# Expert w_down loads in 8 KB runs with every-second-column transposes, 4 KB of DMA scratch, and a fifth ring3 block

## The chip, the cores and the metric

The kernel runs on one core of a Trainium2 chip. The metric is the device time of one execution in microseconds (us), as the median of several runs; the profile is of one such execution. The core's engines are named as in the profile: PE (matmuls) with its weight loads PEld, DVE, ACT, POOL and SP. SP does no arithmetic here: its queue issues most of the DMAs, strictly one after the other. A "q" behind an engine's name (SPq, POOLq) marks what its sequencer issues or waits for.

## What is computed

One layer of a hybrid decoder for 512 prompt tokens and 32 sample tokens: RMSNorm, one input projection, dilated attention, a convolution module, attention into 256 memory tokens, a gated merge with output projection, and then a mixture of 32 experts with top-1 group and top-2 experts in it. Everything up to the experts is the same before and after, so only the last part of the reference is given:

```python
D_MODEL, N_EXPERTS, EXPERT_FF = 1024, 32, 512

def hier_moe(h, lw):
    lg = h @ lw['w_router_group'] + lw['b_router_group']
    pg = softmax(lg); pg_top, g_idx = top_k(pg, 1)
    le = einsum('nd,gde->nge', h, lw['w_router_expert']) + lw['b_router_expert']
    pe = softmax(le of the chosen group); pe_top, e_idx = top_k(pe, 2)
    w = pg_top * pe_top / sum(pe_top)
    gates = one_hot(g_idx * 8 + e_idx) weighted by w          # (544 tokens, 32 experts)
    y = zeros_like(h)
    for e in range(N_EXPERTS):
        hid = silu(h @ lw['w_expert_gate'][e]) * (h @ lw['w_expert_up'][e])
        y = y + gates[:, e:e + 1] * (hid @ lw['w_expert_down'][e])
    return y
```

All data are 32-bit floats. The weights of one expert are 1024x512 (gate), 1024x512 (up) and 512x1024 (down), 2 MB each.

## The kernel before

The kernel runs the whole layer up to the output projection first (the mixer), then the routing, then the 32 experts. Each expert takes up to 64 tokens; tokens beyond that would go to a loop at the end (`For_i` over `n_ovf`), which in the profiled execution makes no pass.

**Weights.** `expert_w(e, alloc)` takes six blocks of [128, 2048] floats (1 MB each) and loads into them, in this order, two halves of gate, two of up and two of down (g0, g1, u0, u1, d0, d1). Loads are numbered through here: load 6e is g0 of expert e, load 6e + 5 its d1, and 191 is the last. A gate or up block gives each partition four rows of 512 floats that lie together in memory, one run of 8 KB. A down block gives partition p the rows p and p + 128 of its half of w_down: two runs of 4 KB.

**Blocks.** `mraw()` hands out blocks in a fixed round: 4 of `ring2`, 2 of `ring2b`, 1 of `ring2c`, 6 of `ring`, 4 of `ring3` (in the order `ORD3`), 2 of `ring4`, 2 of `ring5`, 21 in all. So load j can be issued only when load j - 21 has been read for the last time by PE. The pools of `ring3`, `h2`, `ring4` and `ring5` lie one on top of the other on the left side of SBUF, over space that the mixer has left.

**Queue of loads.** `wload` (through `chained`, L573) issues all loads on the SP queue in their order, and its manual dependency (`DEPTH = 4`) makes each load wait until the load four places before it has landed. So at most four loads are in flight.

**One expert** (`expert_mm`): 32 matmuls with the gate blocks into `pg` and 32 with the up blocks into `pu` (L1477); the gather of the next expert's tokens (`chosen`, `gather`: L1296, two sets of PE work, L1301); silu and product into `hs` (L1485, L1486); two PE transposes of `hs` into `ph` (L1489); a copy to `hT` (L1491); 16 matmuls with the down blocks into `pd` (L1495); scaling by the gates into `o` (L1498); and a scatter with addition of 128 half rows into the output, issued by POOL (L1499).

**Overflow tables.** Before expert 14, `overflow_tables()` takes one more block, `scr`, from `ring` alone, so it gets the next block of those six in turn. About 35 DVE instructions (from L1522) work in it and write `novf` (L1530). `nc.values_load(novf...)` then loads that number into a register of every engine, SP included; in the trace SP's part of it shows as L1576.

**Order.** The order of the instructions within each queue is fixed when the kernel is built, by a planner that follows the program with a simulated clock (`TCKW = dict(schedule_with_timeline_sim=True)`); loads stay in their order, but what stands between two of them on SP is the planner's choice. `YENG` puts two of the output stores on SP as well (L1206).

Of the kernel before, what the change touches and what calls it, by code (L numbers as in the profile page):

```python
# [21 lines left out]
P = 128  # L22
# [28 lines left out]
RING2 = 4  # L51
RING2B = 2
RING2C = 1
RING3 = 4
RING4 = 2
RING5 = 2
SPOS = 2
# [7 lines left out]
DEPTH = 4  # L65
NBUSY = (50, 4)
GORD = (4, 0, 1, 2, 3)
ORD3 = (0, 3, 1, 2)
AHJ = 1
NGH = 3  # L70
MVT = {0: "hi"}
# [82 lines left out]
def build(tc, I, O, cols):  # L154
    nc = tc.nc
    stack = ExitStack()

    def pool(name, bufs=1, space=None, side="left"):
        kw = dict(name=name, bufs=bufs, reuse_waits="tile")
        if space is not None:  # L160
            kw["space"] = space
        else:
            kw["side"] = side
        return tc.tile_pool(**kw)
# [16 lines left out]
    ident = cp.tile([P, P], F32, name="ident")  # L181
# [7 lines left out]
    def cfs(k):  # L189
        a, n = cf_cols[k]  # L190
        return cf[:, a - CF0:a - CF0 + n]
# [7 lines left out]
    def nm(s):  # L199
        cnt[0] += 1  # L200
        return f"{s}_{cnt[0]}"
# [369 lines left out]
    def chained(dst, src):  # L571
        with tc.issue_after(last_load[0].ins):
            last_load[0] = nc.sync.dma_start(dst, src)  # L573
# [221 lines left out]
    for b in range(DB):  # L795
# [14 lines left out]
        for h in range(4):  # L810
            r = slice(32 * h, 32 * h + 32)
            q = [qm[:, 4 * g + h, :] for g in range(3)]
            nc.tensor.matmul(psA[r], q[1], KT[h], start=False, stop=last, skip_group_check=True)
        for h in range(4):
            r = slice(32 * h, 32 * h + 32)
            q = [qm[:, 4 * g + h, :] for g in range(3)]
            nc.tensor.matmul(psB[r, 0:P], q[0], KT[h][:, 384:], start=False, stop=False, skip_group_check=True)
        for h in range(4):
            r = slice(32 * h, 32 * h + 32)
            q = [qm[:, 4 * g + h, :] for g in range(3)]  # L820
# [351 lines left out]
    for q in range(4):  # L1172
        wh, wl = split(ounits[q])
        for ip in range(2):
# [5 lines left out]
            for g in ([slice(0, 2)] if not SPL[q][ip] else [slice(0, 1), slice(1, 2)]):  # L1180
# [9 lines left out]
                for c in range(2):  # L1190
                    k = 2 * q + c
# [17 lines left out]
    ring3 = moe.enter_context(pool("ring3", 1))  # L1209
    first = {"w%d" % q: ring3.tile([P, 2048], F32, name=nm("w"), tag="w%d" % q) for q in range(RING3)}  # L1210
    h2pool = moe.enter_context(pool("h2", 1))
# [71 lines left out]
    def pick(dst, col):  # L1283
        return V.tensor_tensor(dst, col.to_broadcast([P, 5, CAP]), cfs("iota64").unsqueeze(1).to_broadcast([P, 5, CAP]),
                               op=ALU.is_equal)
# [51 lines left out]
    for v in range(2):  # L1337
        px = mm.tile([P, 2, P], F32, name=nm("mm"), tag="mm")
        for i in GORD:
            for f in range(2):  # L1340
                k = 4 * v + 2 * f
# [68 lines left out]
    wg, wu, wd = I["w_expert_gate"][0], I["w_expert_up"][0], I["w_expert_down"][0]  # L1410
# [3 lines left out]
    def mraw():  # L1414
        q = seq[0] % (RING + RING2 + RING2B + RING2C + RING3 + RING4 + RING5)
        seq[0] += 1
        pl = ring
        for cand, n in ((ring2, RING2), (ring2b, RING2B), (ring2c, RING2C), (ring, RING), (ring3, RING3), (ring4, RING4), (ring5, RING5)):
            if q < n:
                pl = cand  # L1420
                break
            q -= n
        tag = "w%d" % ORD3[q] if pl is ring3 else "w"
        if tag in first:
            return first.pop(tag)
        return pl.tile([P, 2048], F32, name=nm("w"), tag=tag)
# [3 lines left out]
    def wload(dst, src):  # L1430
        chained(dst, src)
        loads.append(last_load[0].ins)
        if len(loads) > DEPTH:
            tc.add_manual_dep(loads[-1], loads[-1 - DEPTH].name,
                              mybir.DependencyInfo(mybir.DependencyClass.Sync, mybir.DependencyReason.DATA),
                              reason="bounded queue")

    def expert_w(e, alloc):
        out = []
        for src in (wg, wu):  # L1440
            for f in range(2):
                t = alloc().rearrange("p (k c) -> p k c", k=4)
                wload(t, src[e].rearrange("(p k) c -> p k c", k=8)[:, 4 * f:4 * f + 4, :])
                out.append(t)
        for f in range(2):
            t = alloc().rearrange("p (k c) -> p k c", k=2)
            wload(t, wd[e].rearrange("(k p) c -> p k c", p=P)[:, 2 * f:2 * f + 2, :])
            out.append(t)
        return out

    def gathered(oh):
        gather(oh, lambda: pm.tile([P, 512], F32, name=nm("px"), tag="px", bufs=1), xg, xT1)
        return xT1
# [6 lines left out]
    def expert(xT, w, gc, idc2, after=None, mid=None, early=None):  # L1460
        with tc.issue_after(after.ins) if after is not None else nullcontext():
            return expert_mm(xT, w, gc, idc2, mid, early)
# [8 lines left out]
    def expert_mm(xT, w, gc, idc2, mid, early):  # L1471
        pgt = pm.tile([P, 256], F32, name=nm("pg"), tag="pg")
        pup = pm.tile([P, 256], F32, name=nm("pu"), tag="pu")
        for ps, ws in ((pgt, w[0:2]), (pup, w[2:4])):
            for k in range(8):
                for f in range(2):
                    last = nc.tensor.matmul(ps[CAP * f:CAP * f + CAP], xT[:, k, :], ws[k // 4][:, k % 4, 256 * f:256 * f + 256],  # L1477
                                     start=(k == 0), stop=(k == 7))
            if early is not None and ps is pgt:
                early(last)  # L1480
        if mid is not None:
            with tc.issue_after(last.ins):
                mid()
        hs = work[:, 512:768]
        nc.scalar.activation(hs, pgt, AF.Silu)  # L1485
        nc.vector.tensor_tensor(hs, hs, pup, op=ALU.mult)  # L1486
        ph = pm.tile([P, 2, P], F32, name=nm("ph"), tag="ph", bufs=1)
        for f in range(2):
            nc.tensor.transpose(ph[:, f, :], hs[:, f * P:(f + 1) * P], ident)  # L1489
        hT = work[:, 768:1024].rearrange("p (f s) -> p f s", f=2)  # L1490
        nc.vector.tensor_copy(hT, ph)  # L1491
        pd = pm.tile([P, 512], F32, name=nm("pd"), tag="pd")
        for kk in range(4):
            for f in range(2):
                last = nc.tensor.matmul(pd[CAP * f:CAP * f + CAP], hT[:, kk % 2, CAP * (kk // 2):CAP * (kk // 2) + CAP],  # L1495
                                 w[4 + kk // 2][:, kk % 2, 512 * f:512 * f + 512], start=(kk == 0), stop=(kk == 3))
        o = work[:, :512]
        nc.vector.tensor_scalar(o, pd, gc, None, op0=ALU.mult)  # L1498
        nc.gpsimd.indirect_dma_start(out=y2, out_offset=bass.IndirectOffsetOnAxis(ap=idc2, axis=0), in_=o,  # L1499
                                     in_offset=None, compute_op=ALU.add)  # L1500
        return last
# [66 lines left out]
    for e in range(NE):  # L1568
        w = expert_w(e, mraw)
        if e == 14:  # L1570
            overflow_tables()
        done = expert(xTs[e], w, gates[:, e:e + 1], ids2[:, e:e + 1], done,
                      (lambda: xTs.append(chosen(e + 1))) if e + 1 < NE else None,
                      tables if e == 0 else None)

    n_ovf = nc.values_load(novf[0:1, 0:1], min_val=0, max_val=MAXOVF)  # L1576
    with tc.For_i(0, n_ovf, 1) as it:
        ev = nc.sync.value_load(ovfe[0:1, ds(it, 1)], min_val=0, max_val=NE - 1)
        idc2 = wk.tile([P, 1], I32, name="oidc2")
        gc = wk.tile([P, 1], F32, name="ogc")  # L1580
        nc.vector.tensor_copy(idc2, ids2[:, ds(it + NE, 1)])
        nc.vector.tensor_copy(gc, gates[:, ds(it + NE, 1)])

        def oraw():
            return ring.tile([P, 2048], F32, name=nm("w"), tag="w")

        out = []
        for src in (wg, wu):
            for f in range(2):
                t = oraw().rearrange("p (k c) -> p k c", k=4)  # L1590
                nc.sync.dma_start(t, src[ds(ev, 1)].rearrange("o (p k) c -> p (o k) c", k=8)[:, 4 * f:4 * f + 4, :])
                out.append(t)
        for f in range(2):
            t = oraw().rearrange("p (k c) -> p k c", k=2)
            nc.sync.dma_start(t, wd[ds(ev, 1)].rearrange("o (k p) c -> p (o k) c", p=P)[:, 2 * f:2 * f + 2, :])
            out.append(t)
        oe = wk.tile([P, 2], F32, name="oe")
        nc.vector.tensor_copy(oe[:, 0:1], ovff[:, ds(it, 1)])
        nc.vector.tensor_copy(oe[:, 1:2], ovfb[:, ds(it, 1)])
        oe1 = wk.tile([P, 32], F32, name="oe1")  # L1600
        pc5 = wk.tile([P, 5, 32], F32, name="pc5")
        pc = wk.tile([P, 5, 1], F32, name="pc")
        nc.vector.tensor_scalar(oe1, cfs("iotab")[:, :32], oe[:, 0:1], None, op0=ALU.is_equal)
        nc.vector.tensor_tensor(pc5, posE, oe1.unsqueeze(1).to_broadcast([P, 5, 32]), op=ALU.mult)
        nc.vector.tensor_reduce(pc[:, :, 0], pc5, AX.X, ALU.add)
        nc.vector.tensor_scalar(pc, pc, oe[:, 1:2], None, op0=ALU.subtract)
        oh = ohs[:, 0]
        pick(oh, pc)
        expert(gathered(oh), out, gc, idc2)
# [34 lines left out]
```

## Time and profile before

| | |
|---|---|
| median of 3 runs (lowest, highest) | 1234.89 us (1234.37, 1235.35) |
| span of the profiled execution, first to last instruction | 1233.3 us |
| mean granted TensorE clock | 0.990 of full speed |
| DMA traffic of the execution | 313.02 MB in 125575 packets |
| busy share of the span: PE, PEld, DVE, ACT, POOL | 94%, 69%, 39%, 25%, 24% |

The profile gives no separate device time for the profiled execution; the runs lie 1.1 to 2.1 us above its span. A busy share is a mean over the whole span, and stages differ: the first 640 us are the mixer, the experts' loads begin at 640.7 us and the first scatter of an expert is at 753.8 us. In the tables below "x" is a count; in a row of waits stand the time in all, the number of waits and the longest.

### The profile page before, as it was taken

To read this page: it belongs to the slowest core of one execution; us is meant where nothing else is said; L and a number is where in the kernel's file an instruction comes from. 1 tells how busy PE (TensorE), PEld (TensorE's weight loads), DVE (VectorE), ACT (ScalarE), POOL (GpSimd) and SP (SyncE) were. 2 spreads that over 40 slices of the span, in tenths; PEclk is the share of its full clock that TensorE was granted. 3 is DMA by queue.
4 is the path that set the end of the run, shared out by engine and by line. 5 is a ranking of instruction groups with operands and counts; after the bars stand their busy time and mean duration, and the time that the engine had idled before them with its cause. 6 is when DMAs were issued, how large, how long until landed. Compare 5 with 4: busy or idle time off the path is not lost. (4 is left out here: it accounts for less than half of the span.)

```text
span 1233.3 us, 22282 instructions
## 1 busy us (share of the span) xinstructions
PE 1157.4 (94%) x9248; PEld 850.2 (69%) x9250; DVE 483.4 (39%) x959; ACT 302.5 (25%) x731; POOL 290.2 (24%) x472
## 2 busy tenths in 40 slices
PE   6999999999999989999999988999999998898884
PEld 6898898989546889999998844555555554444441
DVE  6644434443635879856432263112142121111110
ACT  7434343422322422144332231000000000000000
POOL 5443434530840730213221000111111111111001
PEclk9999999999999989999999998999999999999998
DMA  9995754133647542312328487999999999999994
GB/s 319 228 330 153 228 164 139 43 108 103 239 137 266 184 150 69 103 44 95 137 74 358 154 305 297 388 394 399 401 393 400 397 394 401 403 407 401 402 399 145
DMA packets 125575, 313.02 MB, mean 254 GB/s; under 512 B 12842, under 2 KB 69490, under 8 KB 108833
## 3 DMA queue, kind: packets, MB, share of 16 engines
q1 hardware_dynamic: 115440, 295.58, 64.1%
q0 software_dynamic: 7280, 14.36, 5.2%
q10 hardware_dynamic: 2752, 1.65, 0.5%
q8 instruction: 74, 1.21, 0.4%
q14 instruction: 29, 0.23, 0.1%
HBM read 295.66 MB, written 31.35 MB: 265 GB/s over the span
## 5 line engine op out<-in xcount | busy, mean ns | idle before, releaser
L1499 POOL DMA_INDIRECT out_y_all<-work,ids x32 | 49.6, 1549 | 459.9 <-DVE work L1498 420.3
L664 PE MATMUL mm<-hTh,lo 128*128 128x272 f32 x512 | 148.6, 292 | 0.0
L662 PE MATMUL mm<-hTh,hi 128*128 128x272 f32 x512 | 148.6, 290 | 0.0
L663 PE MATMUL mm<-hTl,hi 128*128 128x272 f32 x512 | 148.5, 290 | 0.0
L1477 PE MATMUL pu<-w,xgT 128*64 128x256 f32 x992 | 115.6, 381 | 17.9 <-DMA w<-in_w_expert_up 16.6
L1495 PE MATMUL pd<-w,work 128*64 128x512 f32 x512 | 119.7, 609 | 1.4 <-DMA w<-in_w_expert_down 1.4
L1477 PE MATMUL pg<-w,xgT 128*64 128x256 f32 x992 | 115.0, 380 | 4.1 <-DMA w<-in_w_expert_gate 2.8
L1477 PEld LDWEIGHTS pu<-w,xgT 128*64 128x64 f32 x992 | 69.1, 137 | 61.2 <-DMA w<-in_w_expert_up 26.6
L238 PE MATMUL mm<-hi,hTh 128*128 128x256 f32 x384 | 110.2, 287 | 0.0
L239 PE MATMUL mm<-lo,hTh 128*128 128x256 f32 x384 | 110.0, 286 | 0.0
L240 PE MATMUL mm<-hi,hTl 128*128 128x256 f32 x384 | 109.8, 286 | 0.0
L1477 PEld LDWEIGHTS pg<-w,xgT 128*64 128x64 f32 x992 | 70.3, 137 | 55.7 <-issue 16.7
L232 DVE TENSOR_TENSOR lo<-w,hi 128x2048 fp32r<-128x2048 f32 (+2 forms) x46 | 82.2, 1803 | 45.9 <-ACT hi L231 45.8
L1486 DVE TENSOR_TENSOR work<-work,pu 128x256 f32<-128x256 f32 x32 | 13.5, 421 | 216.1 <-PE pu L1477 216.1
L662 PEld LDWEIGHTS mm<-hTh,hi 128*128 128x128 f32 x512 | 96.8, 189 | 1.8 <-ACT aS L896 0.8
L663 PEld LDWEIGHTS mm<-hTl,hi 128*128 128x128 f32 x512 | 97.0, 190 | 0.3 <-issue 0.2
L664 PEld LDWEIGHTS mm<-hTh,lo 128*128 128x128 f32 x512 | 96.5, 189 | 0.6 <-issue 0.5
L683 DVE SCALAR_TENSOR_TENSOR cT<-u,cT 128x512 f32<-128x512 f32 x120 | 89.8, 766 | 1.7
L1495 PEld LDWEIGHTS pd<-w,work 128*64 128x64 f32 x512 | 34.4, 139 | 65.1 <-issue 60.1
L1296 PE MATMUL px<-h,ohs 128*64 128x512 f16 x620 | 74.0, 380 | 5.6 <-DVE gates L1373 2.8
L231 ACT CAST hi<-w 128x2048 fp32r<-128x2048 f32 (+2 forms) x50 | 68.0, 1389 | 28.1 <-PE mm L663 24.7
L999 POOL TENSOR_TENSOR z<-z,gth 128x272 f32<-128x272 f32 x32 | 35.7, 1117 | 164.4 <-DVE gth L998 164.4
(452 smaller groups left out, 2114.1 us busy)
## 6 DMA issues: line engine op xcount, KB each, us to landing
w<-in_w_expert_gate SPq DMA_DIRECT2D x64, 1024.0 KB, 11.1
w<-in_w_expert_up SPq DMA_DIRECT2D x64, 1024.0 KB, 10.3
w<-in_w_expert_down SPq DMA_DIRECT2D x64, 1024.0 KB, 11.2
w<-in_w_in SPq DMA_DIRECT2D x30, 512.0 KB, 7.1
w<-in_w_in SPq DMA_DIRECT2D x12, 1024.0 KB, 6.9
out_k_win_sample<-in_cache_k SPq DMA_DIRECT2D x8, 1016.0 KB, 12.7
out_v_win_sample<-in_cache_v SPq DMA_DIRECT2D x8, 1016.0 KB, 14.8
w<-in_cache_k SPq DMA_DIRECT2D x6, 1024.0 KB, 5.8
```

The source lines that it names most:

```text
L231: nc.scalar.copy(hi[:, s], v8(t)[:, s])
L232: last_lo[0] = e.tensor_tensor(lo[:, s], v8(t)[:, s], hi[:, s].bitcast(F32), op=ALU.subtract)
L238: nc.tensor.matmul(ps, xh[k], wh[k], start=(k == 0), stop=False)
L239: nc.tensor.matmul(ps, xh[k], wl[k], start=False, stop=False)
L240: nc.tensor.matmul(ps, xl[k], wh[k], start=False, stop=(k == n - 1))
L662: nc.tensor.matmul(ps, wh[k], xh[k], start=(k == 0), stop=False)
L663: nc.tensor.matmul(ps, wh[k], xl[k], start=False, stop=False)
L664: nc.tensor.matmul(ps, wl[k], xh[k], start=False, stop=(k == n - 1))
L683: nc.vector.scalar_tensor_tensor(cTf[:, c, :NP], u[:, c, j:j + NP], w, cTf[:, c, :NP], op0=ALU.mult, op1=ALU.add)
L1296: nc.tensor.matmul(px[CAP * f:CAP * f + CAP], oh[:, i, :], src[:, 4 * f:4 * f + 4, :], start=(i == GORD[0] and r == 0), stop=(i == GORD[-1 ...
L1477: last = nc.tensor.matmul(ps[CAP * f:CAP * f + CAP], xT[:, k, :], ws[k // 4][:, k % 4, 256 * f:256 * f + 256], start=(k == 0), stop=(k == 7))
L1495: last = nc.tensor.matmul(pd[CAP * f:CAP * f + CAP], hT[:, kk % 2, CAP * (kk // 2):CAP * (kk // 2) + CAP], w[4 + kk // 2][:, kk % 2, 512 * ...
```

## The change

Four edits that belong together:

1. A down block now takes its half of w_down so that partition p gets rows 2p and 2p + 1 of that half: one run of 8 KB in place of two of 4 KB. The same in the overflow loop.
2. Rows 2p + k of w_down need columns 2p + k of `hs` on partition p, so each of the two transposes now reads every second column of `hs` (a step of 8 bytes) in place of 128 adjacent ones.
3. `RING3 = 5`, with its new block last in `ORD3`: the round has 22 blocks, and load j waits for the reads of load j - 22.
4. The scratch that SBUF keeps for the descriptors of POOL's DMAs is given as 4096 bytes of each partition. It was not given before, which reserves 16384.

```diff
-RING3 = 4
+RING3 = 5
...
-ORD3 = (0, 3, 1, 2)
+ORD3 = (0, 3, 1, 2, 4)
...
         for f in range(2):
             t = alloc().rearrange("p (k c) -> p k c", k=2)
-            wload(t, wd[e].rearrange("(k p) c -> p k c", p=P)[:, 2 * f:2 * f + 2, :])
+            wload(t, wd[e].rearrange("(h p k) c -> h p k c", h=2, k=2)[f])
...
         ph = pm.tile([P, 2, P], F32, name=nm("ph"), tag="ph", bufs=1)
-        for f in range(2):
-            nc.tensor.transpose(ph[:, f, :], hs[:, f * P:(f + 1) * P], ident)
+        for k in range(2):
+            nc.tensor.transpose(ph[:, k, :], hs.rearrange("p (q k) -> k p q", k=2)[k], ident)
...
-            nc.sync.dma_start(t, wd[ds(ev, 1)].rearrange("o (k p) c -> p (o k) c", p=P)[:, 2 * f:2 * f + 2, :])
+            nc.sync.dma_start(t, wd[ds(ev, 1)].rearrange("o (h p k) c -> (o h) p k c", h=2, k=2)[f])
...
-    nc = bacc.Bacc("TRN2", target_bir_lowering=False, num_devices=1)
+    nc = bacc.Bacc("TRN2", target_bir_lowering=False, num_devices=1, dynamic_dma_scratch_size=4096)
```

## Rows read from the trace of the kernel before

**Rows 1.** Windows: busy time of each engine, granted clock, DMA share, GB/s.

```profile
700.00:752.00 52.00, 44.11 (x320) 25.02 (x321) 29.18 (x88) 18.10 (x29) 2.38 (x6) 0.93 0.66 244
...
800.00:900.00 100.00, 97.45 (x761) 53.25 (x759) 18.84 (x35) 7.18 (x15) 10.79 (x7) 1.00 1.03 400
...
1100.00:1200.00 100.00, 87.23 (x644) 43.79 (x646) 16.00 (x30) 5.82 (x12) 9.25 (x6) 1.00 1.03 402
```

**Rows 2.** Waits of SP from 800 to 1195 us, the queue of the loads.

```profile
SPq L573 <- DMA w<-in_w_expert_down: 119.8, 47, 3.7
...
SPq L1576 <- DVE w L1531: 5.4, 1, 5.4
```

**Rows 3.** Timeline of POOL: scatters of experts 2, 19 and 29 (start, duration).

```profile
783.54 1.55 POOL L1499 DMA_INDIRECT out_y_all<-work,ids  x1 [12.46 <-DVE work L1498]
...
1022.61 1.54 POOL L1499 DMA_INDIRECT out_y_all<-work,ids  x1 [12.50 <-DVE work L1498]
...
1186.81 1.54 POOL L1499 DMA_INDIRECT out_y_all<-work,ids  x1 [14.73 <-DVE work L1498]
```

**Rows 4.** Waits of PE from 1000 to 1234 us.

```profile
PE pu L1477 <- DMA w<-in_w_expert_up: 16.6, 22, 1.7
```

**Rows 5.** Timeline of SP from 1050 to 1100 us: issues of loads (start, duration of both).

```profile
1066.04 2.88 SPq L573 DMA_DIRECT2D w<-in_w_expert_up  x2
1071.08 2.88 SPq L573 DMA_DIRECT2D w<-in_w_expert_down  x2
1076.06 3.26 SPq L573 DMA_DIRECT2D w<-in_w_expert_gate  x2
1082.40 2.88 SPq L573 DMA_DIRECT2D w<-in_w_expert_up  x2
```

**Rows 6.** DMA view, 800 to 1200 us: packets by size; landing of the scatters.

```profile
DMA packets 30975, 159.74 MB, mean 399 GB/s; under 512 B 2751, under 2 KB 2751, under 8 KB 18518
...
out_y_all<-work,ids POOLq DMA_INDIRECT x26, 9.1
```

**Rows 7.** Timeline of SP from 720 to 800 us: four pairs of loads.

```profile
720.03 11.09 SPq L573 DMA_DIRECT2D w<-in_w_expert_up  x2
...
736.66 13.90 SPq L573 DMA_DIRECT2D w<-in_w_expert_gate  x2
752.76 3.73 SPq L573 DMA_DIRECT2D w<-in_w_expert_up  x2
...
776.67 4.46 SPq L573 DMA_DIRECT2D w<-in_w_expert_gate  x2
```

**Rows 8.** Waits of SP from 640 to 800 us.

```profile
SPq L573 <- PE pd L1495: 22.0, 5, 13.1
...
SPq L573 <- PE pg L1477: 18.7, 7, 10.3
```

**Rows 9.** Instructions on w_down: duration min/median/max, first and last start.

```profile
L573 SPq DMA_DIRECT2D w<-in_w_expert_down x64: 378/379/1189, 646.4 to 1204.9; - x64
```

**Rows 10.** Groups of PE instructions by form: transposes, and two moving 128 columns.

```profile
L1489 PE MATMUL ph<-ident,work 128*128 128x128 f32 x64 | 14.0, 301 | 0.6 <-DVE work L1486 0.6
...
L817 PE MATMUL psB<-KT,qpad 128*32 128x128 f32 x64 | 9.6, 273 | 0.0
...
L488 PE MATMUL S<-T 128*32 128x128 f32 x64 | 4.4, 404 | 0.0
```

**Rows 11.** Timeline of DVE: the overflow tables' first instruction, and the write of novf.

```profile
907.14 0.42 DVE L1522 TENSOR_TENSOR w<-cn,cf 128x256 f32<-128x256 f32 x1 [1.19 <-PE pd L1495]
...
910.73 0.15 DVE L1530 CAST novf<-w 128x1 int32<-128x1 f32 x1
```

**Rows 12.** Timeline of SP from 895 to 916 us: the down loads of expert 13.

```profile
905.21 7.00 SPq L573 DMA_DIRECT2D w<-in_w_expert_down  x2
```

**Rows 13.** Timeline of PE from 857 to 870 us: pd of expert 8, pg of expert 9.

```profile
863.04 3.65 PE L1495 MATMUL pd<-w,work 128*64 128x512 f32 x16
...
866.52 3.62 PE L1477 MATMUL pg<-w,xgT 128*64 128x256 f32 x32
```

## The prediction

> **What bounds the kernel now.** I read the windows first, since the shares of the whole span mix stages. From 800 to 1200 us the 16 DMA engines are busy all the time at about 400 GB/s; from 700 to 752 us they move 244 GB/s [rows 1]. So the experts have a DMA limit behind 800 us and something else before it. The waits of SP say what. From 800 to 1195 us its load queue waits almost only for earlier loads to land, 119.8 us of it for down loads [rows 2]: a block is always free, and the next load waits for its turn among four in flight. From 640 to 800 us long waits are for PE, 13.1 and 10.3 us at worst [rows 8]: no block is free.
>
> PE itself is not late at first. Scatters of experts 2 and 19 stand 239.07 us apart, 17 experts at 14.06 us; experts 19 to 29 take 164.20 us, 16.42 each [rows 3]. PE runs ahead on stocked weights until about 1022 us, then takes DMA's pace, and waits 16.6 us for up blocks alone [rows 4]. The last load is issued at 1204.9 us [rows 9], and what follows it (last matmuls, scatter, drain) is a fixed tail of 28.4 us to the end of the span. So the end is set by when DMA has moved the last block: the time at which its stream becomes continuous, plus what is left then.
>
> **Start of the continuous stream.** The two up loads at 720.03 us last 11.09 us together, the gate pair at 736.66 lasts 13.90: in both the second load had no block until PE had read one [rows 7, 8]. At 752.76 and 776.67 the pairs come closer, and from about 776.67 (load 36) on PE frees blocks faster (14.06 us for six) than DMA fills them.
>
> **Price of one load.** Each issue marks the landing of the load four places before, so issue times give the time that DMA spends on each load. In rows 5 the second issue of a pair starts at its start plus the pair's duration less one issue (0.33 for up, 0.34 for gate, 0.38 for down). That gives 1066.04 (d0 landed), 1068.59 (d1), 1071.08 (g0), 1073.58 (g1), 1076.06 (u0), 1078.98 (u1), 1082.40 (next d0) [rows 5]: d1 2.55, g0 2.49, g1 2.50, u0 2.48, u1 2.92, d0 3.42 us. The last two carry a scatter; undisturbed loads would make 15.1 us of the six, the sum is 16.36, so a scatter takes about 1.2 us of DMA. A down load costs 2.55, a gate or up load 2.49: in 8 KB runs 0.055 us less for the same megabyte. The packet counts fit the runs: 30975 - 18518 = 12457 packets of 8 KB or more [rows 6], about 128 for each of the 97 gate and up loads in that window, so down loads go in 4 KB packets.
>
> **The change, part by part.**
>
> *Down loads in 8 KB runs.* From load 36 to 191 there are 26 experts, 52 down loads. At 0.055 us each that is 52 x 0.055 = 2.9 us. Lower bound: nothing, if the 0.055 belongs to w_down itself and not to its runs. Upper bound: the new down block is one contiguous megabyte, where a gate block takes every other 8 KB; should that reach 2.43 us (a megabyte at 431 GB/s, my estimate, 8% over the 400 GB/s of rows 1), it is 52 x 0.12 = 6.2 us. I take 2.9, since the gate load is the nearest row. The Trainium skill's page "DMA: Bandwidth & Descriptors" (Specifications) speaks against this part: it has line rate reached from 512 bytes on, and by it this term is 0. The Trainium skill, in the section Bandwidth of that page, counts some 10.5 ns for a packet, by which eight packets fewer on each engine save 0.084 us a load, an estimate of 4.4 us in all.
>
> *The 22nd block.* Load 21 no longer waits for block 0 (read by PE from about 730 us) but follows load 20 at about 722 us, into time in which DMA has nothing to do [rows 7]. From there each load takes the release that belonged to the one before it: at about 750 us load 26 goes where 25 went, at 776.67 load 37 where 36 went. PE's early pace is not changed, so the continuous stream starts with one load fewer ahead of it: 2.5 us. Lower bound nothing, if the fifth `ring3` block comes free late or another wait eats it; more than one load it cannot be. I take 2.5.
>
> *Transposes of every second column.* 64 instructions of 301 ns. No row has a step of two. Below, nothing; above, the dilated matmul that moves 128 columns at a step of four, 404 ns, against 273 ns for 128 adjacent ones [rows 10]: 131 ns, or 0.26 us an expert. I take nothing for the path either way: 32 x 0.26 = 8.4 us of PE time is covered by the 16.6 us in which PE waits for weights. What shows is at most 0.26 us for each of the three experts that release blocks before 776 us and once in the tail, 1.0 us in all.
>
> *Scratch of 4 KB.* It could make POOL wait for room. A scatter lands 9.1 us after its issue [rows 6] and the next comes 14 us later [rows 3], so there is one at a time: nothing. In the mixer no row can tell; I take nothing there. Everything on the left of SBUF moves down by 12 KB (above `ring3` by 4 KB), further from the right side; nothing again. An uncertainty of +-1 us for the planner's new order goes into the range.
>
> *What moves with it.* `scr` takes the next block of `ring` behind expert 14's loads. With 21 blocks that is the block of load 70 (d0 of expert 11), with 22 that of load 73 (g1 of expert 12). So the tables start later by half a pd and a pg: 3.65 / 2 + 3.62 = 5.4 us [rows 13], at about 912.5 for 907.14, and novf is there at about 916.3 for 910.9 [rows 11]. SP holds a wait for it between d0 and d1 of expert 13, 5.4 us long [rows 2, 12]. Behind it stand all later loads; it costs little because four loads in flight last some 10 us. On PE and DVE the late tables disturb an expert that runs ahead of DMA.
>
> **Sum.** -2.9 - 2.5 = -5.4 us on the profiled span of 1233.3, 1227.9. The median of the runs is 1.6 us above that span and I carry this over: 1234.9 - 5.4 = 1229.5 us, 0.44% faster. About 0.2%, 2.5 us, is what a measurement of this kernel can tell from no change.
>
> **Rivals.**
>
> *Run length is nothing.* Only the block counts: 1234.9 - 2.5 = 1232.4. For it, the 0.055 us is small and rests on one matrix against two others; against it, it returns in every undisturbed pair. The Trainium skill's rule of 512 bytes ("DMA: Bandwidth & Descriptors", Specifications) would end here too. Chance 0.14.
>
> *The block gives nothing.* A wait on what lay under the fifth `ring3` block, or on `ring5` at 720 us, keeps the stream's start: 1234.9 - 2.9 = 1232.0. Against it, there are some 10 us of idle DMA to catch up in. Chance 0.08.
>
> *SP's wait for novf starves DMA.* If the planner leaves SP's register load between expert 13's down loads, SP comes there about 3.4 us sooner (2.5 for the block, 0.9 for 16 down loads), at 901.8, and novf comes at 916.3. Four loads and perhaps a scatter last 10.0 to 11.2 us, so DMA stands still for 3.3 to 4.5 us, and up to another load's 2.5 until it is full again. It decides from 10 us of waiting on. That loses 3.3 to 7.0, say 6.0: 1229.5 + 6.0 = 1235.5, and the whole may end slower than before. Against it: the planner's clock also sees novf late and loads early, and would move the wait two or three loads on, where it stays near 5.4 us, at most 8. Chance 0.12.
>
> *PE becomes the bound.* With 5.4 us gone PE has 11.2 us left to lose, 0.35 us an expert; the step of four gives 0.26. To be slower than before it takes over 0.52 us, a transpose almost twice as long: 1237 at 0.6 us. Chance 0.02.
>
> **How the numbers follow.** The likeliest case, both gains, has 0.60: 1229.5, by its bounds 1226.2 (6.2 + 2.5) to 1231.5 (1.0 for the transposes and 1.0 for the order). The remaining 0.04 is a new order of the mixer that I can't foresee, either way. The range must leave out no more than 0.2, so it goes from 1226.0, over both halves of a gain at 1232, up to the middle of the novf rival: 1226.0 to 1235.0. Faster by over 0.2% (under 1232.4): 0.60, 0.08 and about half of the first rival, with the unforeseen taken off, 0.73. Within 0.2%: the other half and part of the novf case, 0.16. Slower: the rest of that case, PE's and part of the unforeseen, 0.11.
>
> **What would show it.** Right: landings of down loads 2.49 to 2.50 us apart; packets fewer by 8192 in all; the load at about 722 us and everything behind 776 us a place on; the last load issued near 1199.5 us; PE's waits for weights smaller by some 5 us; scatters of experts 2 to 19 still 14.0 us apart. Wrong: down landings at 2.55 or more, transposes past 430 ns, SP waiting over 10 us for novf with a dip of the DMA rate beside it, or the mixer's end moved from where the first expert load at 640.7 us puts it.

## The result, and the profile after

The changed kernel takes 1223.07 us (median of 4 runs, 1222.73 to 1223.19), the kernel before 1234.63 on the same chip: ratio 0.9904, 95% interval [0.9892, 0.9916]. It is 11.6 us faster. 1229.5 was forecast, with a range of 1226.0 to 1235.0: the direction was right, the gain twice as large, and the time lies 2.9 us below the range.

**Up to the last load it went as forecast.** Instructions on w_down in the kernel after, columns as in [rows 9]:

```profile
L573 SPq DMA_DIRECT2D w<-in_w_expert_down x64: 327/328/1187, 645.9 to 1199.6; - x64
```

The last load is issued at 1199.6 us for 1204.9 [rows 9]; "near 1199.5" was forecast. The SP timeline of the kernel after shows both terms of it. First the early stretch, which answers to [rows 7]:

```profile
716.57 3.27 SPq L573 DMA_DIRECT2D w<-in_w_expert_up  x2
...
734.42 2.06 SPq L573 DMA_DIRECT2D w<-in_w_expert_gate  x2
749.71 2.64 SPq L573 DMA_DIRECT2D w<-in_w_expert_up  x2
...
772.91 3.44 SPq L573 DMA_DIRECT2D w<-in_w_expert_gate  x2
```

The pair of loads 20 and 21 takes 3.27 us for 11.09: load 21 no longer waits for PE. Load 25 goes out with its pair at 734.42, and it is load 26 that waits until 749.71. Load 36 is issued at 772.91 for 776.67. Then an undisturbed stretch, which answers to [rows 5]:

```profile
1078.88 2.79 SPq L573 DMA_DIRECT2D w<-in_w_expert_up  x2
1083.82 2.84 SPq L573 DMA_DIRECT2D w<-in_w_expert_down  x2
1088.82 2.94 SPq L573 DMA_DIRECT2D w<-in_w_expert_gate  x2
1094.98 2.83 SPq L573 DMA_DIRECT2D w<-in_w_expert_up  x2
```

Read as before, with 0.33 us for each issue: d1 lands 1078.88 + 2.79 - 0.33 - 1078.88 = 2.46 us after d0, g0 2.48 after d1, g1 2.51, u0 2.49. The down load costs no more than the others; the six take 16.10 us with a scatter among them, for 16.36. The page's line of packets agrees, 8193 fewer than the 125575 of before:

```profile
DMA packets 117382, 313.02 MB, mean 256 GB/s; under 512 B 12841, under 2 KB 69489, under 8 KB 92448
```

**The rest is behind the last scatter.** POOL's timeline of the kernel after, to be read beside [rows 3] (experts 2, 19, 29 and 31):

```profile
782.80 1.55 POOL L1499 DMA_INDIRECT out_y_all<-work,ids  x1 [12.47 <-DVE work L1498]
...
1021.98 1.55 POOL L1499 DMA_INDIRECT out_y_all<-work,ids  x1 [12.48 <-DVE work L1498]
...
1182.70 1.54 POOL L1499 DMA_INDIRECT out_y_all<-work,ids  x1 [14.51 <-DVE work L1498]
...
1213.68 1.54 POOL L1499 DMA_INDIRECT out_y_all<-work,ids  x1 [13.24 <-DVEq L1577]
```

Experts 2 to 19 keep their pace, 239.18 us for 239.07. The last scatter is at 1213.68, and the span ends at 1221.4: 7.7 us. In the kernel before the last scatter stood here, 13.8 us ahead of the end of the span:

```profile
1219.47 1.54 POOL L1499 DMA_INDIRECT out_y_all<-work,ids  x1 [13.91 <-DVEq L1577]
```

What fills that end are instructions of POOL's sequencer on L1638 and L1577, behind the loop. The profile calls them DRAIN and INC_SWDGE_SEM; no row tells what they do inside (columns: duration in ns min/median/max, first and last start). Kernel before:

```profile
L1638 POOLq DRAIN  x3: 46/109/7100, 1225.3 to 1233.0; - x3
...
L1577 POOLq INC_SWDGE_SEM  x1: 1896/1896/1896, 1220.0 to 1220.0; - x1
```

Kernel after:

```profile
L1638 POOLq DRAIN  x3: 46/109/852, 1219.7 to 1221.1; - x3
...
L1577 POOLq INC_SWDGE_SEM  x1: 366/366/366, 1214.2 to 1214.2; - x1
```

One DRAIN took 7.10 us and takes 0.85. Nothing runs beside it, as the window over the long one in the kernel before shows (columns as in [rows 1]):

```profile
1225.40:1232.40 7.00, 0.00 (x0) 0.00 (x0) 0.00 (x0) 0.00 (x0) 0.00 (x0) 0.50 0.00 0
```

The difference of 6.25 us is the part that was not forecast. (INC_SWDGE_SEM shrinks too, but runs while the last scatter is still landing.)

**The waits.** SP from 800 to 1195 us, answering to [rows 2], and PE from 1000 us on, to [rows 4], in the kernel after:

```profile
SPq L573 <- DMA w<-in_w_expert_down: 114.0, 46, 4.1
...
SPq L1576 <- DVE w L1531: 8.5, 1, 8.5
```

```profile
PE pu L1477 <- DMA w<-in_w_expert_up: 14.5, 20, 1.7
```

DMA is still the limit. PE's waits for up blocks shrank by 2.1 us, where the forecast's sign of being right was some 5. SP's wait for novf grew from 5.4 to 8.5 us. The transposes, answering to [rows 10], and their weight loads, which took 140 ns before:

```profile
L1489 PE MATMUL ph<-ident,work 128*128 128x128 f32 x64 | 16.3, 336 | 0.6 <-DVE work L1486 0.6
```

```profile
L1489 PEld LDWEIGHTS ph<-ident,work 128*128 128x128 f32 x64 | 10.1, 206 | 14.8 <-issue 13.4 <-DVE work L1486 1.0 <-DVE w L1542 0.4
```

### The profile page after: what moved, and what is told of

Same layout as the page of the kernel before. It is cut to its first block, busy times and chain, and to the rows that moved or that the text cites. A ratio compares the mean times of both kernels' runs of the same rounds, so it can differ in the third digit from the quotient of the medians.

```text
span 1221.4 us, 22282 instructions
## 1 busy us (share of the span) xinstructions
PE 1157.7 (95%) x9250; PEld 853.9 (70%) x9250; DVE 483.6 (40%) x959; ACT 303.0 (25%) x731; POOL 290.0 (24%) x472
## 3 DMA queue, kind: packets, MB, share of 16 engines
q0 software_dynamic: 7280, 14.36, 5.3%
## 5 line engine op out<-in xcount | busy, mean ns | idle before, releaser
L1477 PE MATMUL pu<-w,xgT 128*64 128x256 f32 x992 | 115.3, 381 | 15.8 <-DMA w<-in_w_expert_up 14.5
```

## The experiments

**One part alone, or one left out.** The theory after the result: three independent gains, runs and block as forecast, and the scratch by way of the DRAIN. The rival: the end of the kernel got shorter because the runs or the block left less to drain. The scratch alone, on the kernel before:

```diff
-    nc = bacc.Bacc("TRN2", target_bir_lowering=False, num_devices=1)
+    nc = bacc.Bacc("TRN2", target_bir_lowering=False, num_devices=1, dynamic_dma_scratch_size=4096)
```

> The kernel before with nothing but the DMA scratch at 4096 bytes. Theory S (the scratch's size sets how long POOL's last DRAIN takes: 7.10 us in the profile before, 0.85 after): DRAIN near 0.85 us, last scatter to the end of the span 7.7 us for 13.8, the last load still issued near 1204.5, time 1228.4, 6.2 us less. Rival R (the end is shorter because w_down's packets or the fifth block changed what is still to be drained): DRAIN stays at 7.1 us and the time at 1234.6.

Measured: 1229.08 us against 1234.75, ratio 0.9957 [0.9944, 0.9971]; last load at 1204.0 us, last scatter 7.8 us ahead of the end, and the DRAIN:

```profile
L1638 POOLq DRAIN  x3: 46/109/852, 1224.3 to 1225.7; - x3
```

The scratch does it, with nothing else changed.

The same line with 8192:

> The kernel before with the DMA scratch at 8192 bytes. Theory S in its plain form (so much of DRAIN's time for each byte): DRAIN 2.9 us by a line through 0.85 us at 4096 and 7.10 at 16384, time about 1230.5. A form of S with a threshold (a ring that is never used beyond some size costs a whole clean-up): DRAIN either 0.85 or 7.1. Rival R: 7.1 us and 1234.6.

Measured: DRAIN 1.873 us; 1229.73 us, ratio 0.9957 [0.9943, 0.9971]. More than at 4096, and less than a straight line between 0.85 and 7.10 gives (2.9). It is neither of the two values that the form with a threshold has.

The runs and transposes without the block and the scratch, which is the diff above without its lines on `RING3`, `ORD3` and `dynamic_dma_scratch_size`:

> The change without its fifth ring3 block and with the scratch as before: runs of 8 KB and transposes of every second column alone. Prediction's term: 52 loads x 0.055 us = 2.9 us less, 1231.7; last load issued near 1202. Rival (run length is nothing): 1234.6 or a little over, since the transposes take 334 ns for 301. Rival R of the shorter end: DRAIN 0.85 us and 1225.5; theory S: DRAIN 7.1 us.

Measured: 1231.01 us against 1234.75, ratio 0.9971 [0.9962, 0.998], so 3.7 us where 2.9 was forecast and nothing was the rival's. The last load is issued at 1199.4 us, sooner than the 1202 expected, in an execution that is the fastest of the ten (1229.46 us). The DRAIN has the length of before:

```profile
L1638 POOLq DRAIN  x3: 46/109/7100, 1219.7 to 1227.4; - x3
```

The block with the scratch that makes room for it:

```diff
-RING3 = 4
+RING3 = 5
-ORD3 = (0, 3, 1, 2)
+ORD3 = (0, 3, 1, 2, 4)
...
+    nc = bacc.Bacc("TRN2", target_bir_lowering=False, num_devices=1, dynamic_dma_scratch_size=4096)
```

> The kernel before with the fifth ring3 block and the scratch of 4096 bytes that makes room for it, w_down and transposes as before. Prediction's term for the block 2.5 us, and theory S 6.2 us: 1225.9, the last load issued near 1202.4. If the block gives nothing: 1228.4, as with the scratch alone.

Measured: 1226.09 us, ratio 0.9939 [0.9926, 0.9953]; last load at 1201.7 us, 2.3 before that of the scratch alone. By medians the block is worth 1229.08 - 1226.09 = 3.0 us, though the intervals of the two ratios just touch, and the runs on top of it 1226.09 - 1223.07 = 3.0. These steps lead from the one kernel to the other, so 5.7 + 3.0 + 3.0 = 11.7 us proves nothing about their independence. The runs measured alone make it 5.7 + 3.0 + 3.7 = 12.4 for 11.6, a difference within the noise.

The block gives less once the runs are 8 KB long. No run has the runs and the scratch without the block; 1231.01 less 6.25 us of DRAIN gives 1224.8, an estimate, so that 1.7 us are left for the block. In the traces, load 36 comes 132.7 us after the first load in the changed kernel for 135.9 with the runs alone, 3.2 less; but the last load comes 559.3 us after the first for 560.0, only 0.7 less. Of the 2.5 us lost between, 1.6 lie from load 78 to 96 (51.41 us for 49.80), where SP waits for novf, 8.5 us for 6.8. In the two kernels below without that wait, a_novf_late and a_best, the last load comes 557.0 and 558.5 us after the first. These are single traces; that the wait takes back part of the block's gain is likely by them, its size is not measured.

**How far the scratch goes.** The changed kernel with 2048, 1024 and 8192 bytes:

```diff
-num_devices=1, dynamic_dma_scratch_size=4096)
+num_devices=1, dynamic_dma_scratch_size=2048)
```

> The changed kernel with the DMA scratch at 2048 bytes. Theory S, with the sizes so far (DRAIN 0.85 us at 4096, 1.87 at 8192, 7.10 at 16384): DRAIN 0.3 to 0.5 us, time 1222.6. Rival W (a smaller ring makes POOL wait for room while it still issues): scatters over 1.54 us or POOL's stores of the mixer late, the first expert load after 641 us, time over 1223.1.

> The changed kernel with the DMA scratch at 1024 bytes. Theory S: DRAIN 0.2 to 0.4 us, time 1222.5. Rival W is likelier here: if POOL waits for room, its stores in the mixer take longer and the first expert load comes after 641 us; time over 1223.5.

> The changed kernel with the DMA scratch at 8192 bytes, in which the fifth block still fits. Theory S: DRAIN 1.87 us as in the kernel before at this size, time 1224.1, 1.0 us over the changed kernel. If the end went with the block or the runs: 0.85 us and 1223.1.

Measured: 1223.16, 1222.63 and 1223.50 us with DRAINs of 0.934, 0.485 and 1.873 us. Their ratios (0.9902 [0.9884, 0.992], 0.9895 [0.9877, 0.9913], 0.9908 [0.9892, 0.9925]) can't be told from the 0.9904 of 4096. POOL does not wait for room: its scatters still take 1.54 to 1.55 us. The first expert load comes at 640.2, 641.7 and 639.9 us; only that of 1024 bytes is late, by 1.5 us, and a_best below, with 1024 bytes too, has it at 640.0, so the size does not do it. The expectation for 2048 fell: its DRAIN is no shorter than that of 4096. That of 1024 is over the 0.2 to 0.4 us expected, and the 1.0 us expected for 8192 can't be told from nothing.

**What DRAIN goes by.** Two edits of the kernel before: twelve stores moved from POOL to ACT, at 16384 bytes, and a scratch of 12288. Each was timed once, so only its trace is read.

```diff
-                        nc.gpsimd.dma_start(
+                        nc.scalar.dma_start(
                             O["k_win_prompt"][0, 0, ip * 256:(ip + 1) * 256, h, :].rearrange("(i p) d -> p i d", p=P),
                             A[:, :, 1, :])
...
-        nc.gpsimd.dma_start(O["v_win_prompt"][0, 0, :, h, :].rearrange("(i p) d -> p i d", p=P), vh)
+        nc.scalar.dma_start(O["v_win_prompt"][0, 0, :, h, :].rearrange("(i p) d -> p i d", p=P), vh)
```

> The kernel before, scratch as it was (16384 bytes), with the 12 stores of the key and value windows (L435, L462) issued by ACT in place of POOL: POOL's queue then carries less than half of its 7280 packets. Theory S1 (DRAIN goes by the room that was reserved): 7.10 us as before. Rival S2 (it goes by what POOL has issued since it last came round its ring): DRAIN about 3 us.

Measured, with the stores moved: POOL's queue carries 6576 packets for 7280, 704 fewer. (The expectation had them as more than half of the 7280, which was wrong.)

```profile
L1638 POOLq DRAIN  x3: 46/109/6120, 1224.6 to 1231.3; - x3
```

So DRAIN fell by 0.98 us at an unchanged scratch: it does not go by the reserved room alone.

> The kernel before with the DMA scratch at 12288 bytes. S1 in a straight line between 8192 (1.87 us) and 16384 (7.10): DRAIN 4.5 us, span about 1230.7. S2 (455 packets for each of 16 engines in the whole execution, which a ring of 12288 bytes may hold without coming round, as one of 16384 may): 7.1 us, or the 1.9 us of 8192.

Measured: DRAIN 4.446 us, span 1230.0. From 8192 to 16384 bytes the line is straight (1.873, 4.446, 7.100: 2.6 us for each 4096), which theory S1 had; but 4096, 2048 and 1024 (0.852, 0.934, 0.485) lie off it, and the moved stores contradict S1 too. S2 as written fails at 12288. Which rule joins the room and what POOL issued stays open. That DRAIN stands on the path is plain in all fourteen traces: from the start of the last scatter to the end, less DRAIN, it is 6.7 to 7.2 us in every one, with DRAINs from 0.485 to 7.100.

**SP's wait for novf.** The overflow tables before another expert:

```diff
-        if e == 14:
+        if e == 12:
             overflow_tables()
```

> The changed kernel with the overflow tables made before expert 12 in place of 14, so that their block is the last of ring in the round, that of load 56, and SP's wait for novf stands before load 78. Theory N (SP's 8.5 us wait for novf between two gate loads let DMA run empty and costs 1 to 2 us): the wait is gone or under 2 us, loads 82 to 90 take 21.7 us for 23.7, time 1221.3. Rival: four loads in flight cover 8.5 us, the time stays at 1223.1.

Measured: 1238.22 us, ratio 1.0024 [1.0014, 1.0034], 15 us over the changed kernel. The expectation was wrong, and DMA ran empty, as in the forecast's rival; but only 11.8 us of it are the wait for novf. SP from 780 us on waits:

```profile
SPq L573 <- DVE ids L1367: 13.0, 1, 13.0
SPq L1576 <- DVE w L1531: 11.8, 1, 11.8
```

and its timeline has no load between the two pairs:

```profile
882.61 2.83 SPq L573 DMA_DIRECT2D w<-in_w_expert_down  x2
911.07 1.12 SPq L573 DMA_DIRECT2D w<-in_w_expert_gate  x2
```

After the wait for novf the next load (78) waited for its own block, that of load 56, in which the tables still worked on DVE. Together 24.8 us of waiting, and 15.1 us were lost. The changed kernel, against which that is counted, loses time to its own wait of 8.5 us; against the next kernel, which has none, it is 1238.22 - 1221.78 = 16.4. So the four loads in flight covered some 8 us, not the 10 that four times 2.5 us would be.

The register load behind the last expert load instead:

```diff
-    n_ovf = nc.values_load(novf[0:1, 0:1], min_val=0, max_val=MAXOVF)
+    with tc.issue_after(last_load[0].ins):
+        n_ovf = nc.values_load(novf[0:1, 0:1], min_val=0, max_val=MAXOVF)
```

> The changed kernel with the register load of novf placed behind the last expert load on SP, everything else as it was. Theory N (SP's wait of 8.5 us for novf lets DMA run empty): loads 78 to 96 take 49.8 us for 51.4, the last load is issued near 1197.7, time 1221.3, 1.5 to 2.1 us under the changed kernel. Rival (the four loads in flight cover it): loads 78 to 96 still 51.4 us, time 1223.1. If the register load at the end stands on the path: its own 0.5 us more.

Measured: SP's wait is gone, and the last load is issued at 1197.7 us for 1199.6. SP of the kernel after, then of this one:

```profile
905.98 10.04 SPq L573 DMA_DIRECT2D w<-in_w_expert_gate  x2
```

```profile
905.91 2.80 SPq L573 DMA_DIRECT2D w<-in_w_expert_gate  x2
```

The windows from 910 to 918 us, whose last three columns are granted clock, DMA share and GB/s, show what stood still, the kernel after first:

```profile
910.00:918.00 8.00, 7.70 (x71) 4.63 (x66) 6.26 (x27) 0.97 (x2) 0.68 (x1) 1.00 0.78 256
```

```profile
910.00:918.00 8.00, 7.67 (x66) 4.42 (x64) 7.29 (x30) 0.97 (x2) 0.00 (x0) 1.00 1.04 386
```

130 GB/s over 8 us are 1.04 MB, one load. Loads 78 and 96 are the first of these pairs, in the kernel after and in this one:

```profile
889.42 2.94 SPq L573 DMA_DIRECT2D w<-in_w_expert_gate  x2
...
940.83 3.06 SPq L573 DMA_DIRECT2D w<-in_w_expert_gate  x2
```

```profile
888.71 2.94 SPq L573 DMA_DIRECT2D w<-in_w_expert_gate  x2
...
938.18 2.83 SPq L573 DMA_DIRECT2D w<-in_w_expert_gate  x2
```

From load 78 to load 96 it takes 49.47 us for 51.41. The three other scratch sizes above, with waits of 8.6 to 9.0 us, take 51.27 to 52.55. The time is 1221.78 us, ratio 0.9905 [0.9889, 0.9922], 1.3 us under the changed kernel by medians; but its five runs go from 1220.47 to 1224.51, and the two intervals overlap. The trace shows the gain, the runs can't.

> The same with the DMA scratch at 1024 bytes. Theories S and N together: DRAIN 0.49 us for 0.85, time 1220.9. If POOL waits for room in the small ring: first expert load over 641 us and no gain over 4096 bytes.

Measured: 1221.83 us, ratio 0.9899 [0.9883, 0.9914], DRAIN 0.485 us, loads 78 to 96 49.52 us. No better than the one before it that can be told, and the best that was found together with it.

## Why the prediction was right and wrong

**The bound** was right: the end hung on when DMA had moved the last block. That the last load left 5.3 us sooner, for 5.4 forecast, is in part luck: two gains that were larger together, and a loss that the sum did not have. The first load went out 0.5 us sooner; from it to load 36 took 132.7 us for 136.0, and from load 36 to 191 426.65 for 428.21. Without the wait for novf (a_novf_late) the last is 424.78, so the wait took back about 1.9 us.

**Runs of 8 KB**, 2.9 us: right. 3.7 us alone and 3.0 on top of the rest. From load 96 to 191, 32 down loads, the six kernels with 4 KB runs took 259.63 to 261.67 us, the eight with 8 KB 258.20 to 259.48; the means are 2.1 us apart. From d0's landing to d1's it is 2.55 or 2.56 us in all six and 2.47 to 2.50 in all eight (medians from load 96 on), as long as a gate load. No run shows the 2.43 us of the upper bound, so that a down block is now one contiguous megabyte gave nothing over a gate block that can be seen. The rival that run length is nothing fell. With it fell the Trainium skill's 512 bytes ("DMA: Bandwidth & Descriptors", Specifications) as a rule by which nothing is left to gain above.

**The 22nd block**, 2.5 us: right in its steps, one place on from load 21, and in size with 4 KB runs (3.0 by medians, 2.3 by the last load). In the changed kernel it is less, 0.7 by the loads and about 1.7 by medians: it brings load 36 forward by over 3 us, and part of that seems to go in the longer wait for novf.

**Transposes**: the cover held, PE still waits 14.5 us for up blocks. The price was within its bounds, 35 ns more for an instruction and 66 ns for its weight load. The Trainium skill ("SBUF — State Buffer", Door 1) lets floats be read at a step inside 16 bytes for free; here a step of 8 bytes made the weight load 206 ns for 140, so for this read the measurement decides against it.

**novf**: the mechanism was right, but the sum had its cost at nothing. The tables start when PE is done with g1 of expert 12, at 911.57 us (912.5 was worked out), novf is written at 914.6 (916.3 was), and the wait moved on by two loads, as the text had it for the likeliest case. It came to 8.5 us, not the "at most 8", and cost 1.9 us where the text had nothing below 10: DMA already runs thin before its four loads are gone (the last issue before the wait is at 905.98 us, and the rate is 287 GB/s from 913 to 914 and 156 in the next us).

**The scratch** is the step that failed: "It could make POOL wait for room [...] I take nothing there", and ahead of it the "fixed tail of 28.4 us". The tail was not fixed: from the last load to the end it is 21.8 us now (1221.4 - 1199.6). Its largest single piece, a DRAIN of 7.10 us with nothing beside it, was in the trace of before and was not looked at, since the text followed the loads to the last scatter and took the rest as given. With it the sum is -2.9 - 2.5 - 6.2 = -11.6 us, the measured gain; that it meets it to the tenth is luck, since the other terms and the cost of novf are known to a microsecond at best. Why the scratch sets the length of DRAIN stays open.

## What to carry to other kernels

Read the trace to its last instruction: what the sequencers do behind the last useful work is serial time like any other, and an argument that calls a tail fixed should name its pieces. A reservation (here the scratch for POOL's descriptors) can cost time at the end and not only room. Where one queue issues all loads, what it may wait for is worth the bytes in flight behind it: a wait of 8.5 us lost 1.9 here and one of 24.8 lost 16.4, so 7 to 8 us were covered where four loads of 2.5 us make 10. Gains measured one by one need not add up: the block, worth 3.0 us with the old runs, was worth less with the new ones, in part because it also made SP wait longer for novf.

## What the runs showed that was not expected

POOL's closing DRAIN depends on the scratch: 7.10 us at 16384 bytes, 4.45 at 12288, 1.87 at 8192, 0.85 at 4096, 0.93 at 2048, 0.49 at 1024, the same to the nanosecond in every kernel of one size and one set of POOL DMAs, and 6.12 at 16384 with 704 packets fewer on POOL's queue. None of these sizes lengthened a scatter's issue (1.54 to 1.55 us).
